# The second mixer's 256-column scores as three rounded products, placed behind the attention's projection

## Chip, cores and metric

The kernel runs on one core of a Trainium2 chip. The time of a run is the device time of that core, in microseconds (us); the runs are compared by their median. A separate, profiled execution gives the page, the trace and all times inside the kernel. Engines are named as in the profile: PE is the matrix engine (PEld its weight loads), DVE the vector engine, ACT the scalar engine, POOL the GpSimd engine, SP the engine that issues most transfers.

## The reference

One layer with two mixers over 256 tokens of 1024 features. A normalised and modulated input `h` is multiplied by `w_in`, and the result is cut into the inputs of an attention (`qa ka va za`), of a gated linear recurrence, here called the second mixer (`qm km vm zm om ig fg`), and two gates (`ga gm`). Each mixer's output goes through its own projection, and the gated sum through `w_out`.

```python
h = _rmsnorm(x, norm_w) * (1 + scale) + shift
(qa, ka, va, za, qm, km, vm, zm, om, ig, fg, ga, gm) = jnp.split(h @ w_in, SPLIT_IDX, axis=-1)
...
ya = (ya * jax.nn.silu(za)) @ w_att_proj
qk = jax.nn.silu(_causal_dwconv(jnp.concatenate([qm, km], axis=-1), conv_w, conv_b))
qm, km = jnp.split(qk, 2, axis=-1)
hm = _mlstm_chunkwise(...)              # per step:  s = (q k^T) * d_mat;  num = s v + ...
...
y = jax.nn.sigmoid(ga) * ya + jax.nn.sigmoid(gm) * ym
return x + gate * (y @ w_out)
```

The change concerns `q k^T` of the second mixer: four heads of 256 features, 256 queries and 256 keys, of which the causal half is used.

## The kernel before

**Rounded and low parts.** Nearly all products of the kernel are made in float32r, a rounded float32. To keep accuracy, each operand is split into a rounded part and the remainder (the low part), and a product is the sum of three: rounded by rounded, rounded by low, low by rounded. `hTh` and `hTl` are the two parts of `h`, `wh` and `wl` those of a weight tile. A few small products are made in float32 directly, among them the scores of the attention (`att_qk`, L603, L604) and those of the second mixer (`ml_scores`, L738 to L751).

**Chunks and groups.** After a first phase (normalisation, modulation, the first 1784 columns of `w_in`, up to 51 us) the work is a list of 25 chunks of 512 columns: the rest of ka, then va, za, qm, km, the attention's projection att, zm, vm, om, ga, gm, the second mixer's projection ml, and out, in halves. Each chunk is four groups of two 128-row weight tiles. A group is 24 products of 256 columns (kind `ws`: L988, L990, L991) or 12 of 512 columns (kind `tok`: L981 to L983). Groups are counted by `g`; att is g = 36 to 43, zm is 44 to 51, vm begins at 52. `C` gives a chunk's index, `done(name, half)` the first group after it.

**The order of work** is written out by hand. In the main loop, step g does in turn: `split(g + 4)`, which makes the weight parts for four groups ahead (a cast on ACT, L447, and a subtraction, L451, on DVE, or on POOL for eight groups around the convolutions; five buffers each); on the first group of a chunk the evacuation of the chunk before (`ev_att`, L689; `ev_zm`, L694, both on ACT); then the hooks that `at(step, ...)` has put there; then loads (`pump`, on SP); then the group's products on PE. Every engine works through its own instructions in this order and waits where an operand is not ready.

**The scores.** `ml_scores(h)` makes for one head, in one PSUM tile, the 128x128 product of the late keys with the late queries and the 128x256 product of the early keys with all queries, in float32 and summed over two 128-feature tiles (L744). DVE multiplies the result by the decay matrix `NM` (L746), ACT casts it to the rounded part `SDh` (L750), POOL subtracts for the low part `SDl` (L751). The numerators (`ml_num`, L762 to L764) read these from g = 65 on. The inputs `qm` and `km` come from a convolution on ACT and DVE (`conv`, L673 and L679, and `conv_silu`, L684). Before the change, heads 0 and 1 stand at g = 35 and 36, heads 2 and 3 at g = 39 and 40, three and four groups after their half of km is done.

**Others near the place.** `gate_acc` (L815) multiplies a 128x1024 tile of the gate's weights on DVE; two of them stand at g = 40, 41 and two at g = 48, 49. `ev_vm` sets a few ones with POOL (L700) at g = 56. Tiles named by `slot(tag, ...)` share memory by tag: a new one waits until the last readers of the old one are through. `s2` holds qT, then yal (the attention's low part, read by att), later omt; `s6` holds the gates G, later vml.

Of the kernel before, what the change touches and what calls it, by code (L numbers as in the profile page):

```python
# [9 lines left out]
F32 = mybir.dt.float32  # L10
F32R = mybir.dt.float32r
AF = mybir.ActivationFunctionType
OP = mybir.AluOpType
# [3 lines left out]
S = 256  # L17
# [49 lines left out]
def tile_hybrid(ctx: ExitStack, tc: tile.TileContext, x, c, params2, w_row, ada_mod, ada_gate,  # L67
                w_in, w_att_proj, w_ml_proj, w_out, out):
    nc = tc.nc
# [81 lines left out]
    def modulation_sum(k, s):  # L151
        if s:
            sums[k] = ph.tile([128, 2], F32, name="sums", bufs=2)
        nc.vector.tensor_tensor_reduce(sq, adat[k][:, s], cb, 1.0, 0.0, OP.mult, OP.add, sums[k][:, s:s + 1])  # L154
# [81 lines left out]
    for j in range(4):  # L236
        n, q = divmod(j, 2)
        nc.tensor.matmul(pc[n][:, q * 256:(q + 1) * 256], pick[:, j:j + 1].to_broadcast([128, 128]), cparts,
                         start=q == 0, stop=q == 1, skip_group_check=True)
# [62 lines left out]
    for step in P1_STEPS:  # L302
        op, k = step[0], int(step[1])
        if op == "L":
            next_loads(k)
        else:
# [5 lines left out]
                 c=lambda k: modulation_sum(k, 1), k=lambda k: modulation_sum(k, 0),  # L312
# [30 lines left out]
    C = {}  # L343
# [3 lines left out]
    def done(name, half):  # L347
        return 4 * (C[name, half] + 1)
# [73 lines left out]
    def free(tag):  # L422
        if tag in FREE:
            hl.tile([128, FREE.pop(tag)], F32, name="free_" + tag, bufs=1)

    def slot(tag, shape, dt, name):
        free(tag)
        return hl.tile(shape, dt, name=name, tag=tag, bufs=1)

    def aux(shape):  # L430
        return ps.tile(shape, F32, name="aux", bufs=4)
# [24 lines left out]
    def at(step, fn, *a):  # L456
        hooks.setdefault(step, []).append((fn, a))
# [4 lines left out]
    T = {}  # L462
# [272 lines left out]
            nc.vector.tensor_tensor(T["yl"][:, ks[q]], yf[q], T["yh"][:, ks[q]].bitcast(F32), op=OP.subtract)  # L735


    def ml_scores(h):  # L738
        qm, km = T["qm"], T["km"]
        pa = aux([128, 384])  # L740
        for c0, s0 in ((256, 128), (0, 0)):
            for kt in range(2):
                ct = 2 * h + kt
                nc.tensor.matmul(pa[:, c0:c0 + 256 - s0], km[:, ct, s0:s0 + 128], qm[:, ct, s0:], start=kt == 0,  # L744
                                 stop=kt == 1)
        nc.vector.scalar_tensor_tensor(T["NM"][:, h], pa, MD ** -0.5, T["NM"][:, h], op0=OP.mult, op1=OP.mult)  # L746
        if "SDh" not in T:
            SD = slot("s5", [128, 2, MH, 384], F32R, "SD")
            T["SDh"], T["SDl"] = SD[:, 0], SD[:, 1]
        nc.scalar.copy(T["SDh"][:, h], T["NM"][:, h])  # L750
        nc.gpsimd.tensor_tensor(T["SDl"][:, h], T["NM"][:, h], T["SDh"][:, h].bitcast(F32), op=OP.subtract)  # L751
# [86 lines left out]
    def ev_out(pt, c0, n, t):  # L838
        cs = slice(c0, c0 + n)
        o = hl.tile([128, n], F32, name="o", tag="scr", bufs=2)  # L840
        if c0 < 512:
# [6 lines left out]
              zm=ev_zm, vm=ev_vm, om=ev_om, ga=ev_ga, gm=ev_gm, ml=ev_ml)  # L848
# [25 lines left out]
    for nm in ("qm", "km"):  # L874
        for hf in range(2):
            s = done(nm, hf)
# [3 lines left out]
    for q in range(2):  # L880
        at(done("za", 0) + 1 + q, att_av, 2 * q)
        at(done("za", 1) + 1 + q, att_av, 4 + 2 * q)
    s = done("km", 0)
    at(s + 3, ml_scores, 0)
    at(s + 4, ml_scores, 1)
    s = done("km", 1)
    at(s + 3, ml_scores, 2)
    at(s + 4, ml_scores, 3)
    at(4 * C["att", 0] - 10, gate_init)
    gate_left = {}  # L890
    for q, nm in enumerate(GSEG):
        s = 4 * C[nm, 0] - 4
# [7 lines left out]
    for hp in range(2):  # L900
        s = done("om", hp)
# [29 lines left out]
    for g in range(NG):  # L931
# [32 lines left out]
        for kk in range(2):  # L964
            k = 2 * kp + kk
            first, last = k == 0, k == KT - 1
            if ch["name"] == "out":

                for i in (0, 1):
                    for t, c0 in ((0, 0), (0, 256), (1, 0), (1, 256)):  # L970
                        a = (sh_, sl_)[i][:, k, t * 128:(t + 1) * 128]
                        cs = slice(c0, c0 + 256)
                        for w in (wh, wl)[:2 - i]:
                            nc.tensor.matmul(mmt[ci][:, t, cs], a, w[:, kk, cs],  # L974
                                             start=first and i == 0 and c0 == 0 and w is wh,
                                             stop=last and i == 1 and c0 > 0, skip_group_check=True)
# [7 lines left out]
            else:  # L984
                for i in range(4):
                    cs = slice(i * 128, (i + 1) * 128)
# [68 lines left out]
```

## Time and profile before

| | us |
|---|---|
| median of 3 runs (353.5 to 354.18) | 353.92 |
| the profiled execution | 352.92 |
| its span on the core | 351.1 |
| PE busy | 345.4 |
| DVE busy | 243.6 |
| ACT busy | 209.9 |
| POOL busy | 84.7 |

In the rows of the profile, a line of a timeline gives the start and the length in us, the engine, the line of the kernel, the operation, and what it writes and reads (`out<-in`); `xN` counts merged instructions, and brackets hold the idle time before and who ended it. A row of the chain gives start, length and what was on the path that ended last. A row of a waits table gives the waiter, the one waited for, the total in us, the times and the longest. PE instructions overlap: one that lasts 0.28 us can follow the one before it by 0.11, so PE is counted by the distance of starts.

### The profile page before, as it was taken

What the parts mean: (1) busy time and instruction counts of PE and PEld (TensorE: products, weight loads), DVE (VectorE), ACT (ScalarE), POOL (GpSimd) and SP (SyncE); (2) the same over time, 40 slices, a digit from 0 to 9 for tenths busy, and PEclk for the clock granted to TensorE, in tenths of its full rate; (3) what the DMA queues carried; (4) which work ended last, traced back from release to release, by engine and by line L of the source; (5) the groups of instructions that cost most, each with busy time, mean ns of one, the idle gap of its engine ahead of it and who ended that gap; (6) DMA issues with size and microseconds to landing.
All of it is one profiled execution on the core that took longest, in us unless ns stands there. A gap on an engine that the chain in (4) does not pass through costs nothing.

```text
span 351.1 us, 6143 instructions
## 1 busy us (share of the span) xinstructions
PE 345.4 (98%) x2424; PEld 321.5 (92%) x2424; DVE 243.6 (69%) x367; ACT 209.9 (60%) x327; POOL 84.7 (24%) x77
## 2 busy tenths in 40 slices
PE   8999999999999999999999999999999999999996
PEld 7778889888999999999999888888899999999996
DVE  6989988849984537767774474764475775659961
ACT  4867799976886867674654435545646374443510
POOL 4800007572004152555240000000010420534000
PEclk9999999999999999999999999999999999999999
DMA  7999999995581453493664955649219219262011
GB/s 301 415 415 412 410 391 346 230 250 243 174 313 57 157 203 137 142 375 129 240 241 139 381 199 217 263 151 380 66 27 362 93 56 368 118 245 116 2 62 60
DMA packets 25876, 77.98 MB, mean 222 GB/s; under 512 B 2928, under 2 KB 6008, under 8 KB 25208
## 3 DMA queue, kind: packets, MB, share of 16 engines
q1 hardware_dynamic: 25696, 77.07, 61.0%
q10 hardware_dynamic: 152, 0.53, 0.5%
q8 instruction: 19, 0.31, 0.3%
q14 instruction: 9, 0.07, 0.1%
HBM read 76.14 MB, written 1.45 MB: 221 GB/s over the span
## 4 chain that ended last, share of the span: by engine, by line
PE 92%; DMA 6%; DVE 0%; issue 0%; SPq 0%; DVEq 0%
PE mm L991 15%; PE mm L988 15%; PE mm L990 15%; PE mm L981 9%; PE mm L982 9%; PE mm L983 9%; PE pm L199 6%; DMA adat<-in_ada_mod_dram 4%; PE mm L974 3%; DMA raw<-in_w_row_dram 3%; PE aux L744 1%; PE pg L199 1%; PE mm L1003 1%; PE aux L641 1%; PE mm L1002 1%; PE mm L1001 1%
## 5 line engine op out<-in xcount | busy, mean ns | idle before, releaser
L451 DVE TENSOR_TENSOR wl<-raw,wh 128x1024 fp32r<-128x1024 f32 (+1 forms) x92 | 116.0, 1273 | 65.1 <-ACT wh L447 65.1
L447 ACT CAST wh<-raw 128x1024 fp32r<-128x1024 f32 (+1 forms) x100 | 102.2, 1031 | 56.7 <-PE mm L983 29.0
L988 PE MATMUL mm<-hTh,wh 128*128 128x256 f32 x320 | 90.1, 282 | 0.0
L990 PE MATMUL mm<-hTl,wh 128*128 128x256 f32 x320 | 88.7, 277 | 0.0
L991 PE MATMUL mm<-hTh,wl 128*128 128x256 f32 x320 | 88.7, 277 | 0.0
L988 PEld LDWEIGHTS mm<-hTh,wh 128*128 128x128 f32 x320 | 60.2, 188 | 0.1
L990 PEld LDWEIGHTS mm<-hTl,wh 128*128 128x128 f32 x320 | 60.2, 188 | 0.1
L991 PEld LDWEIGHTS mm<-hTh,wl 128*128 128x128 f32 x320 | 60.2, 188 | 0.0
L981 PE MATMUL mm<-wh,hTh 128*128 128x512 f32 (+1 forms) x144 | 55.0, 382 | 0.0
L983 PE MATMUL mm<-wh,hTl 128*128 128x512 f32 (+1 forms) x144 | 54.4, 378 | 0.0
L982 PE MATMUL mm<-wl,hTh 128*128 128x512 f32 (+1 forms) x144 | 54.3, 377 | 0.0
L983 PEld LDWEIGHTS mm<-wh,hTl 128*128 128x128 f32 x144 | 27.0, 188 | 5.1
L981 PEld LDWEIGHTS mm<-wh,hTh 128*128 128x128 f32 x144 | 27.0, 188 | 4.7
L982 PEld LDWEIGHTS mm<-wl,hTh 128*128 128x128 f32 x144 | 27.1, 188 | 4.6
L451 POOL TENSOR_TENSOR wl<-raw,wh 128x1024 fp32r<-128x1024 f32 x8 | 19.5, 2458 | 18.4 <-ACT wh L447 18.4
L781 POOL TENSOR_SCALAR f<-f 128x4 f32<-128x4 f32 x2 | 0.4, 198 | 86.9 <-DVE f L780 86.9
L183 ACT CAST wrh<-raw 128x512 fp32r<-128x512 f32 (+1 forms) x24 | 16.2, 689 | 5.0 <-DMA raw<-in_w_row_dram 5.0
L988 PE MATMUL mm<-yah,wh 128*128 128x256 f32 x64 | 18.3, 286 | 0.0
L188 DVE TENSOR_TENSOR wrl<-raw,wrh 128x512 fp32r<-128x512 f32 (+1 forms) x24 | 18.0, 775 | 0.1
L154 DVE CUSTOM_DVE_ANT_0 sq<-adat,cb 128x1024 f32<-128x1024 f32 x14 | 17.1, 1219 | 0.9 <-DMA adat<-in_ada_mod_dram 0.9
L991 PE MATMUL mm<-yah,wl 128*128 128x256 f32 x64 | 17.7, 277 | 0.0
L990 PE MATMUL mm<-yal,wh 128*128 128x256 f32 x64 | 17.7, 277 | 0.0
(220 smaller groups left out, 670.0 us busy)
## 6 DMA issues: line engine op xcount, KB each, us to landing
raw<-in_w_in_dram SPq DMA_DIRECT2D x36, 1024.0 KB, 4.9
adat<-in_ada_mod_dram SPq DMA_DIRECT2D x16, 512.0 KB, 8.2
raw<-in_ada_gate_dram SPq DMA_DIRECT2D x4, 1024.0 KB, 5.3
raw<-in_w_att_proj_dram SPq DMA_DIRECT2D x4, 1024.0 KB, 5.6
raw<-in_w_ml_proj_dram SPq DMA_DIRECT2D x4, 1024.0 KB, 5.4
raw<-in_w_out_dram SPq DMA_DIRECT2D x4, 1024.0 KB, 6.8
raw<-in_w_row_dram SPq DMA_DIRECT2D x15, 256.0 KB, 7.5
raw<-in_w_row_dram SPq DMA_DIRECT2D x7, 384.0 KB, 7.9
```

What stands on the lines that cost most here:

```text
L154: nc.vector.tensor_tensor_reduce(sq, adat[k][:, s], cb, 1.0, 0.0, OP.mult, OP.add, sums[k][:, s:s + 1])
L183: copy(wsp[k][0][:, c0:c1], wrow[k][:, c0:c1])
L188: e.tensor_tensor(l[:, cs], wrow[k][:, cs], h[:, cs].bitcast(F32), op=OP.subtract)
L199: nc.tensor.matmul(pm[ch][:, t], a[:, k, t * 128:(t + 1) * 128], b[:, cs], start=k == 0 and i == 0 and (ch < 3 or t == 0), stop=k == KT - ...
L447: nc.scalar.copy(h, w)
L451: e.tensor_tensor(l, w, h.bitcast(F32), op=OP.subtract)
L981: nc.tensor.matmul(o, a, wh[:, kk], start=first, stop=False)
L982: nc.tensor.matmul(o, a, wl[:, kk], start=False, stop=False)
L983: nc.tensor.matmul(o, b, wh[:, kk], start=False, stop=last)
L988: nc.tensor.matmul(o, wh[:, kk, cs], sh_[:, k], start=first and i % 2 == 0, stop=False, skip_group_check=True)
L990: nc.tensor.matmul(o, wh[:, kk, cs], sl_[:, k], start=False, stop=False, skip_group_check=True)
L991: nc.tensor.matmul(o, wl[:, kk, cs], sh_[:, k], start=False, stop=last and i % 2 == 1, skip_group_check=True)
```

## The change

The two 256-column products of each head (early keys with all queries) are no longer float32: `ml_split(half)` makes rounded and low parts of `km` (the early 128 keys) and `qm` for two heads, with casts on ACT and subtractions on POOL, and `ml_scores` makes three float32r products of them per feature tile. The 128x128 products stay float32. The four heads' steps stand now in the zm segment: `ml_split(0)` at g = 44, heads 0 and 1 at 46 and 47, `ml_split(1)` at g = 48, heads 2 and 3 at 50 and 51. The new tiles take the memory tags `s6` (kms, both halves) and `s2` (qms, one half at a time).

```diff
+    def ml_split(half):
+        qm, km = T["qm"], T["km"]
+        cs = slice(4 * half, 4 * half + 4)
+        if half == 0:
+            T["kms"] = slot("s6", [128, 2, 2, 4, 128], F32R, "kms")
+        qs, ks = slot("s2", [128, 2, 4, S], F32R, "qms"), T["kms"][:, half]
+        T["qms"] = qs
+        for hl_, src in ((ks, km[:, cs, 0:128]), (qs, qm[:, cs])):
+            nc.scalar.copy(hl_[:, 0], src)
+            nc.gpsimd.tensor_tensor(hl_[:, 1], src, hl_[:, 0].bitcast(F32), op=OP.subtract)
+
     def ml_scores(h):
         qm, km = T["qm"], T["km"]
         pa = aux([128, 384])
-        for c0, s0 in ((256, 128), (0, 0)):
-            for kt in range(2):
-                ct = 2 * h + kt
-                nc.tensor.matmul(pa[:, c0:c0 + 256 - s0], km[:, ct, s0:s0 + 128], qm[:, ct, s0:], start=kt == 0,
-                                 stop=kt == 1)
+        for kt in range(2):
+            ct = 2 * h + kt
+            nc.tensor.matmul(pa[:, 256:384], km[:, ct, 128:], qm[:, ct, 128:], start=kt == 0, stop=kt == 1)
+        qs, ks = T["qms"], T["kms"][:, h // 2]
+        for kt in range(2):
+            c = 2 * (h % 2) + kt
+            for i, j in ((0, 0), (0, 1), (1, 0)):
+                nc.tensor.matmul(pa[:, 0:256], ks[:, i, c], qs[:, j, c], start=kt + i + j == 0, stop=kt == 1 and i == 1)
...
-    s = done("km", 0)
-    at(s + 3, ml_scores, 0)
-    at(s + 4, ml_scores, 1)
-    s = done("km", 1)
-    at(s + 3, ml_scores, 2)
-    at(s + 4, ml_scores, 3)
+    s = 4 * C["zm", 0]
+    for half in range(2):
+        at(s + 4 * half, ml_split, half)
+        at(s + 4 * half + 2, ml_scores, 2 * half)
+        at(s + 4 * half + 3, ml_scores, 2 * half + 1)
```

## The prediction

> **What bounds the kernel now.** I read the page first (engines, chain), then what TensorE waits for, then the chain in order of time.
>
> ```profile
> span 351.1 us, 6143 instructions
> PE 345.4 (98%) x2424; PEld 321.5 (92%) x2424; DVE 243.6 (69%) x367; ACT 209.9 (60%) x327; POOL 84.7 (24%) x77
> PE 92%; DMA 6%; DVE 0%; issue 0%; SPq 0%; DVEq 0%
> ```
>
> ```profile
> PE warm L230 <- POOL ident masks.py:199: 1.4, 1, 1.4
> PE pm L199 <- DVE wrl L188: 1.1, 2, 0.7
> PE pc L238 <- DVE cparts L127: 0.2, 1, 0.2
> ```
>
> TensorE (PE) is 98% busy and makes 92% of the chain. The second fence is everything PE waits for, 2.7 us in all, and every line of it belongs to the first phase (L238 and below). From the first group of the main loop to the end PE never waits. Two things follow. Each PE microsecond that the change saves there is saved from the span, since nothing else is late. And each microsecond that PE is made to wait there is added, since nothing later gives it back.
>
> **The PE work.** Chain rows first: start, length, line, count.
>
> ```profile
> 62.48 0.87 PE aux L491 x8
> 73.33 0.43 PE aux L603 x2
> 159.00 1.31 PE aux L744 x8
> 163.13 1.31 PE aux L744 x8
> 172.62 1.31 PE aux L744 x8
> 176.76 1.31 PE aux L744 x8
> 326.23 10.88 PE mm L974 x96
> ```
>
> ```profile
> 245.95 0.28 PE L762 MATMUL aux<-vaug,SD 128*128 128x258 f32 x1
> 247.02 0.40 PE L981 MATMUL mm<-wh,hTh 128*128 128x512 f32 x1
> ```
>
> One float32 product shows as two instructions (the x2 of L603 is one call, the x8 of L744 are four). 128 columns cost 0.87/8 = 0.109 us per instruction, 256 columns 0.43/2 = 0.215. One head of the scores (L744) is four of each, 4 x 0.109 + 4 x 0.215 = 1.30, which is the 1.31 of the chain. A float32r product of 256 columns costs 10.88/96 = 0.113 in a long run, and 0.119 in the short blocks between 512-column groups ((247.02 - 245.95)/9, the numerator products). The new head keeps the four 128-column instructions and has six float32r ones: 4 x 0.109 + 6 x 0.119 = 1.15. I take the short block, because the new scores stand between 512-column groups too. Four heads fall from 5.24 to 4.60: 0.64 saved.
>
> There is a second, smaller gain. Between the first two blocks lie 163.13 - 159.00 - 1.31 = 2.82 us for a group of 24 float32r products, which at 0.113 is 2.72; likewise 176.76 - 172.62 - 1.31 = 2.83. These two groups run 0.10 us slow after a float32 block. In a 512-column group such an overhead has no room, so I count 0.21 gained, with 0 to 0.35 as its bounds. Sum: **0.85 us saved**, between 0.64 (no second gain) and 1.0 (0.113 for the products).
>
> [...]
>
> **What is added and moved.** Per half (two heads), `ml_split` puts on ScalarE (ACT) a cast of 128x512 (k) and one of 128x1024 (q), and on GpSimd (POOL) a subtraction of each. The nearest rows are the same operations on the same sizes (min/median/max ns), then the ACT queue around the new place, and POOL's neighbours:
>
> ```profile
> L648 ACT CAST yah<-yf x4: 607/620/622, 109.1 to 127.1; 128x512 fp32r<-128x512 f32 x4
> L649 POOL TENSOR_TENSOR yal<-yf,yah x4: 1297/1306/1307, 109.8 to 127.8; 128x512 fp32r<-128x512 f32 x4
> L451 POOL TENSOR_TENSOR wl<-raw,wh x8: 2391/2403/2839, 129.0 to 165.6; 128x1024 fp32r<-128x1024 f32 x8
> L751 POOL TENSOR_TENSOR SD<-NM,SD x4: 1011/1022/1442, 164.6 to 180.8; 128x384 fp32r<-128x384 f32 x4
> ```
>
> ```profile
> 180.21 0.51 ACT L750 CAST SD<-NM 128x384 fp32r<-128x384 f32 x1 [0.85 <-DVE NM L746]
> 188.94 1.05 ACT L447 CAST wh<-raw 128x1024 fp32r<-128x1024 f32 x1 [1.68 <-PE mm L990]
> 189.90 1.01 ACT L689 COPY attT<-mm 128x1024 f32<-128x1024 f32 x1
> 194.47 1.05 ACT L447 CAST wh<-raw 128x1024 fp32r<-128x1024 f32 x1 [1.62 <-PE mm L983]
> 197.19 1.05 ACT L447 CAST wh<-raw 128x1024 fp32r<-128x1024 f32 x1 [1.67 <-PE mm L983]
> 199.91 1.05 ACT L447 CAST wh<-raw 128x1024 fp32r<-128x1024 f32 x1 [1.67 <-PE mm L983]
> 200.87 1.02 ACT L694 ACTIVATE zmt<-mm 128x1024 f32<-128x1024 f32 x1
> ```
>
> ```profile
> 188.81 0.40 PE L981 MATMUL mm<-wh,hTh 128*128 128x512 f32 x1
> 199.71 0.39 PE L981 MATMUL mm<-wh,hTh 128*128 128x512 f32 x1
> 205.15 0.39 PE L981 MATMUL mm<-wh,hTh 128*128 128x512 f32 x1
> ```
>
> ```profile
> 180.09 1.28 DVE L815 CUSTOM_DVE_ANT_0 raw<-raw,cbg,prm 128x1024 f32<-128x1024 f32 x1
> 181.86 1.46 DVE L451 TENSOR_TENSOR wl<-raw,wh 128x1024 fp32r<-128x1024 f32 x1 [0.49 <-ACT wh L447]
> 201.00 1.23 DVE L451 TENSOR_TENSOR wl<-raw,wh 128x1024 fp32r<-128x1024 f32 x1 [1.50 <-ACT wh L447]
> 202.14 1.28 DVE L815 CUSTOM_DVE_ANT_0 raw<-raw,cbg,prm 128x1024 f32<-128x1024 f32 x1
> 302.76 2.72 DVE L451 TENSOR_TENSOR wl<-raw,wh 128x1024 fp32r<-128x1024 f32 x1 [1.50 <-ACT wh L447]
> ```
>
> ```profile
> 180.80 1.44 POOL L751 TENSOR_TENSOR SD<-NM,SD 128x384 fp32r<-128x384 f32 x1 [2.21 <-ACT SD L750]
> 302.01 5.72 POOL L836 TENSOR_TENSOR raw<-raw,gateb 128x1024 f32<-128x1024 f32 x2 [12.85 <-DMA gateb<-gd]
> ```
>
> Read the last two fences together. VectorE (DVE) asked at 302.76 for 1.23 us of work and took 2.72: it stood until 304.25, just before POOL's first L836 would end (302.01 + 2.39). POOL's second L836 then needed 3.3 instead of 2.39, because DVE had gone first. So DVE operations like L451 (two inputs in SBUF) and these POOL operations exclude each other for their whole length and take turns. L815 does the same: POOL's row of 180.80 stood until 181.23 (1.44 against 1.01) while DVE's L815 ended at 181.37, so the turn passes 0.14 before the recorded end. PE's consumers allow 5.4 us (two groups of 2.72) from split to scores. That is the cover to test.
>
> *First half*, t = 0 at 188.81, where PE begins the zm segment. The ACT queue holds the wh cast of four groups ahead (from 0.13; it waits for PE to leave a buffer), `ev_att` to 2.10, then the k cast 2.01 to 2.63 (each starts 0.09 before its predecessor's recorded end, as 189.90 does), then the q cast to 3.59. POOL follows an ACT result by 0.08 (180.21 + 0.51 to 180.80): k's low part 2.71 to 4.01, q's low part 4.0 to 6.4. DVE's wl subtraction of that group is over by 2.45, and the next comes behind the q cast and so finds POOL in its turn: POOL is undisturbed. PE reaches the scores at 5.44, does the 128-column products (0.44) and the one product of the rounded parts (0.11), and at 6.0 needs q's low part. With 0.1 for the hand-over and the weight load, an estimate, **PE waits 0.5 us**.
>
> *Second half*, t = 0 at 199.71. ACT: wh cast from 0.20, `ev_zm` 1.16 to 2.18, k cast 2.09 to 2.71, q cast to 3.67, next wh cast 3.58 to 4.63. DVE: wl 1.29 to 2.52, then `gate_acc` (L815) 2.43 to 3.71. POOL asks for k's low part at 2.79, while L815 has the turn: it runs 3.57 to 4.87. DVE asks for its next wl at 4.67 and gets the turn at 4.73, before POOL can ask for q's low part (4.85): DVE 4.73 to 5.96. q's low part runs 5.82 to 8.22. PE needs it at 6.0: **2.3 us**, counted with the same 0.1. If DVE's request came 0.2 later, POOL would go first, 4.85 to 7.25, and PE would wait 1.4. Both ends go into the range. I take 2.3, since DVE's row 201.00 follows its cast within 0.05, and the ACT times leave it ahead.
>
> The rest costs nothing: the casts behind `ml_split` come up to 1.7 us later, and a cast of 194.47 is used by PE at 205.15, over 9 us on. The same margin covers DVE's wl that POOL keeps waiting, and the ACT cast of the scores (L750), behind which the next wh cast queues while DVE's product and PE's scores finish. Without it, each of these would go straight into PE's wait. The moved steps issue no DMA. They pass two `gate_acc` on DVE, whose input only has to be freed for SP's next load, and POOL's L700, which may now wait for the scores but is wanted five groups later. The score results are first read at 245.95, 14 groups on. At the old place PE had no wait to lose.
>
> Sum: -0.85 + 0.5 + 2.3 = **+2.0 us** (1.95). The profiled execution took 352.92 with a span of 351.1, the median of the runs is 353.92; on the profiled one I expect 354.9, on the median **355.9**.
>
> **The rivals.**
> (B) DVE loses the race in the second half: -0.85 + 0.5 + 1.4 = +1.05, **355.0**. For it: a margin of under 0.2 us between estimates of ACT times. Against: two rows (DVE after cast, cast after predecessor) fix each step.
> (C) The waits do not occur and it is faster: the low parts are ready when PE asks. Place: the (0,1) product at 6.0 of each half; it decides if POOL ends by 5.9. Price 0.85, **353.1**. For it: POOL has nothing else to do there, and each half has 5.4 us of PE work as cover. Against: 3.7 us of POOL work alone, begun at 2.7, already end at 6.4, without any conflict.
> (D) PE's clock drops in the long wait. The trace has a slow pace only at the start:
>
> ```profile
> 1.35 2.50 PE L230 MATMUL warm<-ident 128*128 128x128 f32 x10 [1.35 <-POOL ident masks.py:199]
> 6.87 1.38 PE L262 MATMUL xps<-diag,xt 128*128 128x128 f32 x10
> 26.02 0.74 PE pm L199 x2
> 27.00 3.64 PE pm L199 x16
> ```
>
> Ten products of 128 columns took 2.50 at the start and 1.38 from 6.87 on, so some 5 us ran at half pace, about 2.5 us lost. After the 0.7 us wait before 26.02 the pace was at once the full one (3.64/16 = 0.227). A wait of 2.3 us is not shown; with the clock lost it would be 355.9 + 2.5 = **358.4**. [...]
> (E) In the second half DVE's next `gate_acc` also goes ahead of q's low part (one more turn of 1.28 - 0.14 = 1.14): **357.0**. Against: at 302 the turns alternate.
>
> **How the numbers follow.** Chances: forecast 0.60, B 0.19, C 0.12, D 0.04, E 0.05. The forecast's own range is 355.3 to 356.5 (POOL and ACT times off by 0.2, the gain 0.64 to 1.0). About 0.2%, 0.7 us, is what a measurement of this kernel can tell from no change. C is faster by that in 0.08 and, with a wait left over in one half, within it in 0.04; B with both its waits shorter comes within it in 0.05. So faster 0.08, same 0.09, slower 0.83. The range 354.4 to 357.0 leaves out C and D and a piece of B.
>
> **What the changed profile would show.** PE waits on POOL for the low part of q in two places, 0.5 and 2.3 us; POOL rows near 1.3 and 2.4 us, with the second half's stretched by DVE's; the four score blocks 1.15 us each apart from the wait; no slow group in the attention's projection; full clock. The forecast is wrong if PE shows no wait on POOL, if the second wait is 1.4 (B), or if POOL and DVE overlap without stretching.

## The result

| | before | changed |
|---|---|---|
| median, us | 353.14 (352.62 to 354.18, 8 runs) | 354.92 (354.73 to 356.6, 8 runs) |
| ratio to before, 95% interval | | 1.0062 (1.0040 to 1.0085) |
| the profiled execution | 352.92 | 354.86 |
| its span | 351.1 | 353.1 |

The change makes the kernel slower by 0.6%, about 2.2 us by the ratio and 1.8 us by the two medians. The two profiled spans differ by 2.0 us. The eight runs of the changed kernel fall into two groups: five at 354.7 to 354.95 with a granted PE clock (PE's mean clock over the span, as a share of full speed) of 1.0, and three at 356.4 to 356.6 with 0.995. The profiled execution is one of the five; the three are taken up below.

**The profile after.** First the page and the first line of PE's waits.

```profile
span 353.1 us, 6174 instructions
PE 344.6 (98%) x2432; PEld 320.8 (91%) x2432; DVE 246.5 (70%) x367; ACT 213.3 (60%) x331; POOL 92.1 (26%) x81
```

```profile
PE aux L759 <- POOL qms L747: 2.2, 2, 2.1
```

PE is busy for 0.8 us less than before (344.6 for 345.4) while the span is 2.0 longer. PE has a new wait, twice, for POOL's subtraction in `ml_split` (L747). A PE instruction counts as busy until its modelled end, so the 2.2 us of this view leaves out what overlaps; the full wait is the distance of two starts less the usual 0.113. PE's rows at heads 0 and 2:

```profile
188.71 0.60 PE L754 MATMUL aux<-qmT,kmT 128*128 128x128 f32 x4
189.07 0.36 PE L759 MATMUL aux<-qms,kms 128*128 128x256 f32 x1
189.59 0.86 PE L759 MATMUL aux<-qms,kms 128*128 128x256 f32 x5 [0.16 <-POOL qms L747]
190.28 0.40 PE L994 MATMUL mm<-wh,hTh 128*128 128x512 f32 x1
...
202.37 0.60 PE L754 MATMUL aux<-qmT,kmT 128*128 128x128 f32 x4
202.73 0.36 PE L759 MATMUL aux<-qms,kms 128*128 128x256 f32 x1
205.18 0.86 PE L759 MATMUL aux<-qms,kms 128*128 128x256 f32 x5 [2.08 <-POOL qms L747]
205.87 0.40 PE L994 MATMUL mm<-wh,hTh 128*128 128x512 f32 x1
```

Each time PE does the four float32 instructions and the product of the two rounded parts, and then stands before the product with q's low part: 189.59 - 189.07 - 0.11 = 0.41 us, and 205.18 - 202.73 - 0.11 = 2.34. What POOL, ACT and DVE did ahead of that:

```profile
185.88 1.31 POOL L747 TENSOR_TENSOR kms<-kmT,kms 128x512 fp32r<-128x512 f32 x1 [18.97 <-ACT kms L746]
187.15 2.39 POOL L747 TENSOR_TENSOR qms<-qmT,qms 128x1024 fp32r<-128x1024 f32 x1
...
199.73 2.10 POOL L747 TENSOR_TENSOR kms<-kmT,kms 128x512 fp32r<-128x512 f32 x1 [2.04 <-ACT kms L746]
201.79 3.33 POOL L747 TENSOR_TENSOR qms<-qmT,qms 128x1024 fp32r<-128x1024 f32 x1
```

```profile
197.17 1.05 ACT L447 CAST wh<-raw 128x1024 fp32r<-128x1024 f32 x1 [0.57 <-PE mm L996]
198.13 1.02 ACT L694 ACTIVATE zmt<-mm 128x1024 f32<-128x1024 f32 x1
199.04 0.61 ACT L746 CAST kms<-kmT 128x512 fp32r<-128x512 f32 x1
199.55 1.06 ACT L746 CAST qms<-qmT 128x1024 fp32r<-128x1024 f32 x1
200.50 1.05 ACT L447 CAST wh<-raw 128x1024 fp32r<-128x1024 f32 x1
```

```profile
199.40 1.28 DVE L829 CUSTOM_DVE_ANT_0 raw<-raw,cbg,prm 128x1024 f32<-128x1024 f32 x1
...
201.58 1.33 DVE L451 TENSOR_TENSOR wl<-raw,wh 128x1024 fp32r<-128x1024 f32 x1 [0.90 <-ACT wh L447]
202.84 3.37 DVE L829 CUSTOM_DVE_ANT_0 raw<-raw,cbg,prm 128x1024 f32<-128x1024 f32 x1
```

In the first half POOL needs 1.31 and 2.39 us, undisturbed, and ends at 189.54, 0.05 before PE goes on. In the second half both subtractions are stretched, to 2.10 and 3.33. The first stands behind DVE's `gate_acc` (L829 here, L815 before), which began at 199.40. The second asks at 201.79; DVE's wl subtraction (L451) had asked at 201.58 and goes first. The same rows show the other direction: the `gate_acc` of 202.84 takes 3.37 instead of 1.28, because POOL's turn lies ahead of it.

### The profile page after: what moved, and what is told of

The parts are those of the page before. It is cut to its first block, busy times and chain, and to the rows that moved or that the text cites. A ratio compares the mean times of both kernels' runs of the same rounds, so it can differ in the third digit from the quotient of the medians.

```text
span 353.1 us, 6174 instructions
## 1 busy us (share of the span) xinstructions
PE 344.6 (98%) x2432; PEld 320.8 (91%) x2432; DVE 246.5 (70%) x367; ACT 213.3 (60%) x331; POOL 92.1 (26%) x81
## 4 chain that ended last, share of the span: by engine, by line
PE 78%; issue 7%; DMA 6%; POOL 4%; DVE 3%; ACT 1%; SPq 0%; DVEq 0%; POOLq 0%; ACTq 0%
PE mm L1001 12%; PE mm L1003 12%; PE mm L1004 12%; PE mm L996 8%; PE mm L994 8%; PE mm L995 8%; PE pm L199 6%; DMA adat<-in_ada_mod_dram 4%; PE mm L987 3%; DMA raw<-in_w_row_dram 3%; POOL qms L747 2%; DVE kmT L679 1%; PE pg L199 1%; PE mm L1016 1%; PE aux L641 1%
## 5 line engine op out<-in xcount | busy, mean ns | idle before, releaser
L451 DVE TENSOR_TENSOR wl<-raw,wh 128x1024 fp32r<-128x1024 f32 (+1 forms) x92 | 117.1, 1284 | 66.0 <-ACT wh L447 66.0
L451 POOL TENSOR_TENSOR wl<-raw,wh 128x1024 fp32r<-128x1024 f32 x8 | 19.5, 2461 | 18.4 <-ACT wh L447 12.1
L1001 PE MATMUL mm<-ymh,wh 128*128 128x256 f32 x64 | 17.7, 276 | 0.0
```

Of the source, the lines that this page charges most:

```text
L451: e.tensor_tensor(l, w, h.bitcast(F32), op=OP.subtract)
L1001: nc.tensor.matmul(o, wh[:, kk, cs], sh_[:, k], start=first and i % 2 == 0, stop=False, skip_group_check=True)
```

## The experiments

Each kernel was run beside the kernel before on the same chip, the first four on one chip and the last four on another. Spans are those of the profiled executions; the kernel before had a median of 352.85 us (26 runs) in the first four and 352.92 (17 runs) in the last four.

| kernel | span | median | ratio to before (95%) | PE's waits, us |
|---|---|---|---|---|
| e1_later | 350.6 | 351.97 | 0.9967 (0.9956 to 0.9978) | none |
| e2_gate | 351.2 | 353.28 | 1.0009 (0.9997 to 1.0022) | 0.40 and 0.57 |
| e3_dve | 350.3 | 351.97 | 0.9968 (0.9957 to 0.9980) | none |
| e4_fp32 | 351.2 | 352.93 | 0.9997 (0.9988 to 1.0006) | none |

PE's waits are those for `ml_split`. A tenth execution of e2_gate took 705.72 us at full clock, twice the time of the other nine; its cause is not known, and it is in neither the ratio nor the counts below.

**Later scores.** The same work, with one more group of PE work between split and scores:

```diff
-        at(s + 4 * half, ml_split, half)
-        at(s + 4 * half + 2, ml_scores, 2 * half)
-        at(s + 4 * half + 3, ml_scores, 2 * half + 1)
+        at(s + 6 * half, ml_split, half)
+        at(s + 6 * half + 3, ml_scores, 2 * half)
+        at(s + 6 * half + 4, ml_scores, 2 * half + 1)
```

> The scores come one group later after each split (split at g = 44 and 50, scores at 47, 48, 53, 54), so PE has 8.2 us of other work between split and scores instead of 5.4. Theory (the change loses only by PE's two waits, 0.41 and 2.33 us; its products save 0.85): both waits vanish, the four score blocks stay at about 1.16 us each, span about 350.3, 0.8 us below the 351.1 of the kernel before. Rival (the added casts and subtractions delay the weight parts, and the wait is only where the lost time shows first): PE waits somewhere else, span stays above 352.

PE's rows at head 1; the block of head 0 began at 191.67, and all four blocks look like this one:

```profile
195.58 0.60 PE L754 MATMUL aux<-qmT,kmT 128*128 128x128 f32 x4
195.94 0.96 PE L759 MATMUL aux<-qms,kms 128*128 128x256 f32 x6
196.73 0.40 PE L994 MATMUL mm<-wh,hTh 128*128 128x512 f32 x1
```

The six products follow each other without a gap, 196.73 - 195.58 = 1.15 us a block. Both waits are gone, no other has come, and the kernel is 0.33% faster than before, though it issues every cast and subtraction of the change. So these cost nothing by themselves, and the rival falls: the change loses by the waits alone. The second split also stands further from `gate_acc` here, and POOL takes 1.82 and 2.40 us for it. But the distance alone would have been enough: in the changed kernel q's low part was done at 205.12, and one group later (2.72 us) PE would have asked for it at about 205.6.

**Without the turns.** The two `gate_acc` of that stretch come three groups later, all else as changed:

```diff
-        s = 4 * C[nm, 0] - 4
+        s = 4 * C[nm, 0] - (1 if nm == "vm" else 4)
         at(s, gate_acc, 2 * q)
```

> As the changed kernel, but the two gate_acc of DVE at g = 48 and 49 come three groups later (g = 51 and 52). Theory (turns between DVE and POOL make the second wait long): k's low part runs undisturbed in about 1.3 us, q's low part then gets its turn ahead of DVE's wl and takes 2.4 us, PE's second wait falls from 2.33 to about 0.5, the first stays 0.4, span about 351.3. Rival (POOL's subtraction is slow there for another reason, the casts of ACT or the strided source): q's low part still takes about 3.3 us, the second wait stays above 2, span about 353.

The second half, POOL, then DVE, then PE:

```profile
199.62 1.29 POOL L747 TENSOR_TENSOR kms<-kmT,kms 128x512 fp32r<-128x512 f32 x1 [2.04 <-ACT kms L746]
200.88 2.38 POOL L747 TENSOR_TENSOR qms<-qmT,qms 128x1024 fp32r<-128x1024 f32 x1
```

```profile
201.47 4.01 DVE L451 TENSOR_TENSOR wl<-raw,wh 128x1024 fp32r<-128x1024 f32 x2 [2.09 <-ACT wh L447]
```

```profile
202.62 0.36 PE L759 MATMUL aux<-qms,kms 128*128 128x256 f32 x1
203.31 0.86 PE L759 MATMUL aux<-qms,kms 128*128 128x256 f32 x5 [0.32 <-POOL qms L747]
```

POOL's subtractions take 1.29 and 2.38, as in the first half. Now it is DVE that stands: two wl subtractions need 4.01 us instead of about 2.4. PE's second wait falls from 2.34 to 0.57 (the two starts, unrounded, are 0.686 apart, less 0.113). Nothing of ACT's or POOL's own work was changed for this, so 1.8 us of the second wait came from the turns, and the rest from POOL's 3.7 us of work being too long for the 5.4 us between split and scores.

**q's low part on DVE.**

```diff
-            nc.gpsimd.tensor_tensor(hl_[:, 1], src, hl_[:, 0].bitcast(F32), op=OP.subtract)
+            (nc.vector if hl_ is qs else nc.gpsimd).tensor_tensor(hl_[:, 1], src, hl_[:, 0].bitcast(F32), op=OP.subtract)
```

> As the changed kernel, but q's low part is subtracted on DVE (1.23 us for 128x1024) instead of POOL (2.4). Theory: in the first half it ends about 5.0 us after PE begins the zm segment, before PE asks at 5.9: no wait; in the second half it must let POOL's k part pass and ends at about 5.9: a wait of at most 0.2. Span about 350.5. Rival (DVE is the fuller engine, its own work is pushed back and PE waits for weight parts): PE waits on wl, span above 351.5.

DVE, then PE, in the second half:

```profile
200.18 1.47 DVE L747 TENSOR_TENSOR qms<-qmT,qms 128x1024 fp32r<-128x1024 f32 x1 [1.15 <-ACT qms L746]
201.58 1.27 DVE L829 CUSTOM_DVE_ANT_0 raw<-raw,cbg,prm 128x1024 f32<-128x1024 f32 x1
```

```profile
201.92 0.60 PE L754 MATMUL aux<-qmT,kmT 128*128 128x128 f32 x4
202.28 0.96 PE L759 MATMUL aux<-qms,kms 128*128 128x256 f32 x6
203.07 0.40 PE L994 MATMUL mm<-wh,hTh 128*128 128x512 f32 x1
```

DVE subtracts q's part in 1.47 us, 0.24 of it standing behind POOL's k part, and is through at 201.65; PE needs it at 202.39. No wait is left. The expectation had the second half's q part end later, since it put `gate_acc` ahead of it: in the order of the program `ml_split` comes first, and here `gate_acc` (201.58) queues behind it. The kernel is as fast as with later scores.

**The move alone.** The kernel before, its float32 scores at g = 46, 47, 50, 51 and nothing else:

```diff
-    s = done("km", 0)
-    at(s + 3, ml_scores, 0)
...
+    s = 4 * C["zm", 0]
+    for half in range(2):
+        at(s + 4 * half + 2, ml_scores, 2 * half)
+        at(s + 4 * half + 3, ml_scores, 2 * half + 1)
```

> The kernel before with nothing but the move: the float32 scores stand at g = 46, 47, 50, 51, without splits. Theory (the place is free of cost, and only spares the two groups that ran 0.10 us slow after a float32 block): four blocks of 1.31, no PE wait, span 350.9, 0.2 below 351.1. Rival (the new place itself costs: the queues of ACT and DVE stand behind the scores there): span above 351.5.

```profile
188.87 1.47 PE L744 MATMUL aux<-qmT,kmT 128*128 128x128 f32 x8
189.99 0.58 PE L979 MATMUL mm<-wh,hTh 128*128 128x512 f32 x1
190.41 0.40 PE L980 MATMUL mm<-wl,hTh 128*128 128x512 f32 x1
```

The place costs nothing, and it gives nothing either: 351.2 and 351.1 are the same. The next block begins at 192.95, 4.08 us after this one: 1.31 for the block, 2.72 for the group, and 0.05 over. Before it was 4.13, and the 0.2 expected from the move did not come. So the slow group did not vanish behind this block, it kept 0.05 us of the 0.10; taken four times, an estimate from this one distance, that is the 0.2 of the two slow groups before.

**The length of the wait and the clock.** The three long runs of the changed kernel speak for rival D. To see whether the wait drops the clock, its length was changed. All three start from `e2_gate` and repeat, in the second half, a part of POOL's subtraction with the same result: a 128x128 piece of k ahead of k's low part (w10_part), k's low part (w28_k2, shown), q's low part (w40_q2, with `qs` in place of `ks`). The changed kernel ran again beside them (w23_same).

```diff
-            nc.gpsimd.tensor_tensor(hl_[:, 1], src, hl_[:, 0].bitcast(F32), op=OP.subtract)
+            for _ in range(1 + (half == 1 and hl_ is ks)):
+                nc.gpsimd.tensor_tensor(hl_[:, 1], src, hl_[:, 0].bitcast(F32), op=OP.subtract)
```

> e2_gate with one more POOL subtraction of 128x128 ahead of k's low part in the second half (a repeat of part of it): PE's second wait grows from 0.57 to about 1.0 us. Turns theory: POOL still asks for q's low part ahead of DVE's wl, wait about 1.0, span about 351.6. [...]

> The changed kernel itself, as the point of 2.3 us in this series. Three of its eight runs had a granted clock of 0.995 and a span 1.7 us longer. [...] Rival (it belonged to that chip or that hour): none, or nearly all.

> e2_gate with k's low part of the second half subtracted twice on POOL: PE's second wait about 2.8 us, span about 353.5 where the clock holds. [...]

> e2_gate with q's low part of the second half subtracted twice on POOL, with a turn of DVE between them: PE's second wait about 4.0 us, span about 354.7 where the clock holds. Theory: nearly all runs at 0.995, span about 356.4. [...]

| kernel | PE's longer wait | runs with granted clock 0.995 or less | span of these | span of the others | ratio to before (95%) |
|---|---|---|---|---|---|
| e2_gate | 0.57 | none of 9 | | 351.2 to 352.3 | 1.0009 (0.9997 to 1.0022) |
| w10_part | 1.12 | none of 10 | | 351.8 to 352.1 | 1.0020 (1.0011 to 1.0029) |
| changed and w23_same | 2.34 | 7 of 13 | 354.6 to 355.0 | 352.9 to 353.3 | 1.0062 (1.0040 to 1.0085) and 1.0110 (1.0075 to 1.0145) |
| w28_k2 | 2.88 | 4 of 4 | 355.0 to 355.8 | | 1.0119 (1.0105 to 1.0133) |
| w40_q2 | 3.85 | 4 of 4 (0.989 to 0.990) | 357.1 to 357.5 | | 1.0168 (1.0155 to 1.0181) |

A further execution of w23_same, the profiled one, is left out of the counts (its ratio holds it): its clock was 0.95 from start to end, it was some 3.2 us late before it came to the scores, and its wait of 2.33 us lowered the clock no further. By itself w23_same has 4 of 5; against 3 of 8 before, the numbers are too small to tell chance from a difference of the chip or the hour. One of the 26 runs of the kernel before, which has no such wait, also shows 0.995, with a span of 351.8 for the usual 351.1. No trace of it was kept, and what lowered its clock stays open.

In w28_k2 the drop can be seen in the profile. The stretches (start and end, length, PE busy with its count, granted clock, DMA share, GB/s), then PE's rows:

```profile
202.69:206.11 3.42, 1.24 (x8) 1.00 0.00 0
206.11:209.52 3.41, 2.96 (x10) 0.50 0.00 0
209.52:212.93 3.41, 3.41 (x21) 1.00 0.00 0
```

```profile
206.56 1.44 PE L760 MATMUL aux<-qms,kms 128*128 128x256 f32 x5 [2.63 <-POOL qms L748]
207.80 0.63 PE L995 MATMUL mm<-wh,hTh 128*128 128x512 f32 x1
208.22 0.63 PE L996 MATMUL mm<-wl,hTh 128*128 128x512 f32 x1
208.65 0.63 PE L997 MATMUL mm<-wh,hTl 128*128 128x512 f32 x1
...
209.75 0.40 PE L997 MATMUL mm<-wh,hTl 128*128 128x512 f32 x1
209.98 0.40 PE L995 MATMUL mm<-wh,hTh 128*128 128x512 f32 x1
```

The clock goes to half at 206.11, while PE still waits, and comes back 3.41 us later: 512-column products start 0.43 apart (208.65 - 208.22) until 209.5, then 0.23 as ever. In the changed kernel this costs 1.7 us where it happens (354.8 against 353.1). No trace of those seven executions was kept, so that they lose by the same drop at the same place is inferred from their clock, 0.995 as in w28_k2, and from their length. In w40_q2 the half clock lasts 6.82 us (206.12 to 212.94), which is why its spans are above the 356.4 expected.

In w28_k2's trace PE's last product ended at 203.93 by the record, 2.18 us before the clock fell. In the profiled execution of the changed kernel the wait of 2.34 us holds 2.09 us without work (203.09 to 205.18), and there the clock held:

```profile
202.70:205.20 2.50, 0.42 (x5) 1.00 0.00 0
205.20:208.20 3.00, 3.00 (x16) 1.00 0.30 78
```

The same wait came with full clock in 6 of 13 executions and with 0.995 in 7; what decides between the two is not shown.

The three products at the old place were not tried: there the memory of `qms` (tag s2) is still held by yal.

## Why the prediction was right

The forecast was +1.95 us on the profiled execution and 355.9 for the median, measured were 2.0 and 354.92, against a kernel before whose median had come down from 353.92 to 353.14 with more runs. That fall of 0.78 us is why 354.92 lies below the forecast's own range (355.3 to 356.5) and next to the 355.0 of rival B, and inside the wider one. By the number alone B would fit; the 2.0 us between the profiled executions and the rows decide for the forecast's mechanism. By its own steps:

- *The score block*, 1.15 predicted, is 1.15 (e1_later).
- *The second gain* of 0.21 failed as a term: that such an overhead has no room in a 512-column group was the author's estimate, and in e4_fp32 it was 0.05 after the float32 block of 188.87; in e1_later the distance of two blocks, 195.58 - 191.67 = 3.91, less 1.15 and 2.72 leaves 0.04. So PE's saving is about 5.24 + 0.21 - 4 x 1.19 = 0.7, and not 0.85.
- *The first wait*, 0.5, is 0.41. POOL began 0.07 earlier than worked out (2.64 after PE's group start at 183.24, for 2.71), and the hand-over took less than the 0.1.
- *The second wait*, 2.3, is 2.34, and by the steps named: k's part behind `gate_acc`, DVE's wl ahead of q's part. DVE asked at 201.58 and POOL at 201.79, a lead of 0.21 us; B would have needed that to turn. E did not come either: the `gate_acc` of 202.84 stood behind q's part.
- *The sum*: -0.7 + 0.41 + 2.34 = 2.05, measured 2.0.
- *Full clock* was the step that held only in part. The forecast gave D a chance of 0.04 for a wait of 2.3 us, and it came in 7 of 13 executions. Its price was 1.7, and not 2.5: in w28_k2's trace the clock came back after 3.41 us, where the price of 2.5 was taken from some 5 us of half pace at the start. The trace of the kernel before holds no wait of this length; in w28_k2 2.18 us without a product came ahead of the fall. That five of the first eight runs, the profiled one among them, kept the full clock was luck for the forecast; in w23_same four of five did not. So the forecast of 355.9 lies between the two groups of runs and describes neither: +2.0 is right for the runs at full clock, +3.7 for the others.

C fell as argued: POOL's 3.7 us begun at 2.64 do not fit before 5.9.

## What to carry to other kernels

Where one engine is never late, an added step on idle engines is free only if it ends before that engine asks, so count its queue from the release of its first input: here 0.7 us of saved products lost to 2.7 us of waiting, and one more group of distance, or the faster engine for the larger subtraction, turned +0.6% into -0.3%. Lengths of GpSimd and VectorE operations that take turns must not be read from undisturbed rows alone (here POOL's 2.39 us became 3.33, DVE's 1.28 became 3.37); lay both queues side by side. And look at the granted clock beside a wait of PE: here 2.34 us of waiting came with 0.995 and 1.7 us more in 7 of 13 executions.

## What was not expected of the hardware

With a PE wait of 2.88 us the granted clock was lower in 4 of 4 executions; in the trace of one of them it fell to half for 3.41 us. Beside waits of 2.34 us the granted clock was lower, and the run 1.7 us longer, in 7 of 13, while waits of 0.4 to 1.1 us never did this in 19. The lower clock is the likely reason why the changed kernel has two times, 354.9 and 356.5.
